# The scatters of expert gates: one generator that hands them out at GpSimd's pace, in turns between four sets

## The chip, the cores and the metric

The kernel runs on one core of one Trainium2 chip. The metric is the device time of one execution in microseconds (us). It was timed three times before the change: 3150.28, 3154.98 and 3162.14 us, a median of 3154.98 us. One further execution was profiled; all rows below come from it.

## What is computed

Two transformer blocks over 256 tokens of width 2048, all in float32. The first block's second half is a layer that picks, for each token and each of 8 heads, 16 of 16384 experts:

```python
scores = einsum('thpc,hpnc->thpn', q, sub_keys)      # 8 heads, 2 halves, 128 keys
vals, idx = lax.top_k(scores, 16)
cand = vals[..., 0, :, None] + vals[..., 1, None, :]
top_vals, top_c = lax.top_k(cand.reshape(T, 8, 256), 16)
experts = i1 * 128 + i2                              # 128 experts for each token
gates = softmax(top_vals)
y = einsum('ted,td->te', expert_down[experts], x)    # then gelu, times gates
y = einsum('ted->td', ... expert_up[experts])
```

The kernel does not gather the experts' rows. It multiplies all 16384 experts with all tokens, and then multiplies the activations with a gate that is zero wherever a token did not choose the expert.

## The kernel before, in words

The matrix products run as one long list in `run` (L268): each gemm is cut into weight tiles of 1 MB, each tile into two subtiles. A subtile is loaded by SP (`raw`), split into a rounded part on ACT (`whi`) and a remainder on DVE or GpSimd (`wlo`), and multiplied by TensorE. The program is written out while it is built, in one order for each engine: each subtile's instructions, then one call of `round` (L225), which advances each active generator of each lane by one step. What a generator issues in a step lands on its engine's queue at that place. Each engine runs its queue in order; semaphores are set by the framework from the data. The planner has a clock of its own for each engine, `vt`, which `Meter` (L173) moves on by an estimated time for each instruction. DMAs move no clock.

The gates go like this. `query` and `choose` (L982, L1023) compute, for each of 4 groups of two heads (`g`) and 2 halves of the tokens (`tt`), the 16 best experts and their gates: 8 sets of 32 columns, one after another on DVE. `scatter` (L1091) then issues, for each of a set's 32 columns, one indirect DMA (L1096) that adds 128 gates to a table in DRAM. There are four tables, `gd[g % 2, tt]`; sets 1 to 4 write four different ones, sets 5 to 8 the same four again. An accumulating scatter reads and writes its table, so each waits until the last scatter on the same table has landed. The lane `rows` runs up to four such generators at once, and each gives one scatter in each round.

The expert layer has two parts. `s1` multiplies the 16 chunks of 1024 experts with the tokens (256 subtiles); `activate` writes the activations to DRAM. `s2` multiplies the gated activations with the second weights. Between them stands `weigh` (L1118): for each chunk GpSimd loads the activations (L1124) and four pieces of the gate tables (L1127), adds two of them (L1130), and nine rounds later DVE multiplies activations and gates (L1133). The first `weigh` generators are started when the fourteenth chunk of `s1` has been activated (L940), and only when all 256 scatters have been handed out (L1121). GpSimd's queue holds first the scatters, then loads and additions of chunk 0, then those of chunk 1. In DVE's queue the multiplications stand between the `wlo` of the last subtiles of `s1`. When all scatters are handed out, `share` goes back to 2.0 (L1102); from then on a `wlo` may go to GpSimd when DVE's clock runs 2 us ahead.

Of the kernel before, what the change touches and what calls it, by code (L numbers as in the profile page):

```python
# [10 lines left out]
I32 = mybir.dt.int32  # L11
U32 = mybir.dt.uint32
AF = mybir.ActivationFunctionType
OP = mybir.AluOpType
# [4 lines left out]
T = 256  # L19
# [5 lines left out]
CAND = [(0, 1, 16), (1, 1, 8), (2, 1, 5), (3, 1, 4), (4, 1, 3), (5, 3, 2), (8, 8, 1)]  # L25
NCAND = 50
CLAMP = 2.0
MATCH, PACE = 0.09, 2.0
SWA_ORDER = [0, 3, 1, 4, 2, 5, 6, 9, 7, 10, 8, 11]


# [177 lines left out]
class Build:  # L209
# [364 lines left out]
    def body(self):  # L574
        from contextlib import ExitStack
        with ExitStack() as ctx:
            tc = self.tc
            self.cp = ctx.enter_context(tc.tile_pool(name="cp", bufs=1))
            self.sm = ctx.enter_context(tc.tile_pool(name="sm", bufs=1))
            self.wp = ctx.enter_context(tc.tile_pool(name="wp", bufs=1))  # L580
            self.xp = ctx.enter_context(tc.tile_pool(name="xp", bufs=1))
            self.np = ctx.enter_context(tc.tile_pool(name="np", bufs=1))
            self.wk = ctx.enter_context(tc.tile_pool(name="wk", bufs=1))
            self.hgt, self.hgs = None, deque()
            self.ph = None
            self.ps = ctx.enter_context(tc.tile_pool(name="ps", bufs=1, space=PSUM))
            self.dr = ctx.enter_context(tc.tile_pool(name="dr", bufs=1, space=DRAM))
            ctx.enter_context(tc.manual_schedule())
            self.xs = Slots(self.xp, "xt", 3)
            self.nb = Slots(self.np, "nb", 7)  # L590
            self.lane("evac", 2, 2)
            self.lane("main", 8, 1)
            self.lane("tail", 4, 4)
            self.lane("attn", 2, 1)
            self.lane("choose", 1, 1, True)
            self.lane("top", 2, 2, True)
            self.lane("rows", 4, 2)
            self.program()
            self.phase(None)

# [282 lines left out]
    def peer(self, hn, st):  # L883
        nc, ins = self.nc, self.ins
        nch = NE // CH
        x = self.x_of(hn)
        topn = set()
        done = dict(rows=0)
        at, acts, ws = {}, {}, []
        s2 = [0]  # L890

        def begin():
            assert not any(self.lanes[l]["queue"] or self.lanes[l]["active"] for l in ("attn", "tail"))
            self.phase("query")
            self.share = 1e9
            p = self.pp
            st["keys"] = self.nb.take([128, 2048])
            nc.gpsimd.dma_start(st["keys"], ins["keys"])
            st["top"] = self.nb.take([128, 3, 2, 8, 2, 16])
            st["pick"] = self.nb.take([128, 768])  # L900
            st["pk"] = st["pick"][:, :512].rearrange("p (t i n) -> p t i n", t=2, i=2)
            st["v"], st["ixf"] = st["top"][:, 0], st["top"][:, 1]
            st["ix"] = st["top"][:, 2].bitcast(U32)
            self.eqs = Slots(p, "eq", 2)
            st["oh"] = self.xs.take([128, 4096])
            st["q"], st["qT"], st["sc"] = (deque(st["oh"][:, 512 * i:512 * i + 512] for i in r)
                                           for r in ((0, 1, 2, 3), (4, 5), (6, 7)))

        def q_evac(g, acc):
            for tt in range(2):  # L910
                self.until(lambda: st["q"])
                q = st["q"].popleft()
                nc.scalar.activation(q, acc[tt], AF.Copy, scale=st["rh"][:, tt:tt + 1])
                self.add("top", self.query(g, tt, q, st, topn))
                self.add("choose", self.choose(g, tt, st, topn, done))

        def s1_evac(c):
            def f(g, acc):
                if c not in acts:
                    acts[c] = self.dr.tile([8, 128, T], F32, name=f"act{c}")  # L920
                self.until(lambda: "rrow" in st)
                sg = self.tmp([128, 2, T])
                for n in range(2):
                    nc.scalar.activation(sg[:, n], acc[n][:, T:], AF.Copy)
                self.add("evac", activate(c, g % 4, acc, sg))
            return f

        def activate(c, j, acc, sg):

            yield 1  # L930
            for n in range(2):
                nc.vector.tensor_tensor(sg[:, n], sg[:, n], acc[n][:, :T], op=OP.add)
            nc.vector.tensor_tensor(sg, sg, st["rrow"][:, None, :].to_broadcast([128, 2, T]), op=OP.mult)
            yield 1
            nc.scalar.activation(sg, sg, AF.Gelu_apprx_tanh)
            yield 1
            nc.scalar.dma_start(acts[c][2 * j:2 * j + 2].rearrange("a p t -> p a t"), sg)
            if j == 3:
                ws.append(self.weigh(c, acts, at, st, done, s2))
                if c >= nch - 3:  # L940
                    while ws:
                        self.add("main", ws.pop(0))

        def s2_evac(c):
            def f(g, acc):
                for tt in range(2):
                    hs = self.h[:, tt, 512 * g:512 * g + 512]
                    nc.vector.tensor_tensor(hs, hs, acc[tt], op=OP.add)
                if c == nch - 1 and "after_peer" in st:
                    for tt in range(2):  # L950
                        self.add("main", st["after_peer"](g, tt))
            return f

        def s2_done(c):
            def f():
                at[c].free()
                s2[0] = c + 1
            return f

        def s1_done():  # L960
            for hf in hn:
                hf.free()
            self.nb.give(st["pick"])
            if "rows_2" in st:
                self.add("main", st["rows_2"]())

        def x_at(c, kc):
            return (at[c], kc) if c in at and at[c].n[kc] == 2 else None

        g = [Gemm("query", ins["wq"], 0, range(4), 4, x, q_evac, None, begin)]  # L970

        def s1(c):
            return Gemm("s1", ins["wd"], 0, range(4 * c, 4 * c + 4), 2, x, s1_evac(c),
                        s1_done if c == nch - 1 else None, turned=True)

        def s2g(c):
            return Gemm("s2", ins["wu"], 8 * c, range(4), 2,
                        lambda kc: x_at(c, kc), s2_evac(c), s2_done(c))

        return g + [s1(c) for c in range(nch)] + [s2g(c) for c in range(nch)]  # L980
# [42 lines left out]
    def choose(self, g, tt, st, topn, done):  # L1023

        nc, p = self.nc, self.pp
# [10 lines left out]
        for src, dst in ((v, cand), (ixf, ec)):  # L1036
            o = 0
# [15 lines left out]
        tv, tf, tp, e, gs = tt4[:, 0], tt4[:, 1], tt4[:, 2].bitcast(U32), tt4[:, 3], tt4[:, 4]  # L1053
# [32 lines left out]
        nc.vector.tensor_scalar(ix, e.rearrange("p a b -> p (a b)"), 128.0, self.c("row"), op0=OP.mult, op1=OP.add)  # L1086
        if g == 3 and tt == 1:
            self.nb.give(st["top"])
        self.add("rows", self.scatter(g, tt, st, done))

    def scatter(self, g, tt, st, done):  # L1091

        nc = self.nc
        gd = st["gd"][g % 2, tt].rearrange("e (t o) -> (e t) o", o=1)
        for c in range(32 * g, 32 * g + 32):
            nc.gpsimd.indirect_dma_start(  # L1096
                out=gd, out_offset=bass.IndirectOffsetOnAxis(ap=st["pk"][:, tt, 0, c:c + 1].bitcast(I32), axis=0),
                in_=st["pk"][:, tt, 1, c:c + 1], in_offset=None, compute_op=OP.add)
            yield 1
        done["rows"] += 32  # L1100
        if done["rows"] == T:
            self.share = 2.0  # L1102

    def zero_gates(self, st):

# [605 lines left out]
```

## Time and profile before

| | us |
|---|---|
| median of three runs | 3154.98 |
| the profiled execution, whole | 3151.58 |
| its span, first to last instruction | 3149.8 |
| TensorE busy | 3056.1 (97%) |
| DVE busy | 2008.5 (64%) |
| ACT busy | 1429.5 (45%) |
| GpSimd (POOL) busy | 744.8 (24%) |

An engine's busy time is a sum over stages with different limits, so a mostly idle engine can still be the one that the others wait for in one stage. TensorE is idle for some 94 us of the span; where that falls is read from the windows.

### The profile page before, as it was taken

The numbers are of one execution on the slowest core, as the hardware profiler recorded it, in microseconds if no ns is written. First come the engines' busy times: TensorE is split into PE (matmuls) and PEld (weight loads), VectorE is DVE, ScalarE is ACT, GpSimd is POOL, SyncE is SP. The second block draws the span as 40 slices with busy tenths as digits, with TensorE's granted clock in tenths as the row PEclk, the third lists the DMA queues.
The fourth block names the chain that finished last, engine by engine and source line by source line (L and its number), as shares of the span: only waits on it lengthen the run. The fifth ranks groups of instructions, "written<-read, shape, count | busy, mean of one in ns | idle before, by whom it ended". The sixth has DMA issues, their size and how long they took to land.

```text
span 3149.8 us, 39414 instructions
## 1 busy us (share of the span) xinstructions
PE 3056.1 (97%) x15388; PEld 2574.3 (82%) x15388; DVE 2008.5 (64%) x2908; ACT 1429.5 (45%) x1918; POOL 744.8 (24%) x503
## 2 busy tenths in 40 slices
PE   8999999999999995699999999999999999999998
PEld 6888888888888884678888888877888888888887
DVE  4555668999555552677676765655757555555565
ACT  4445444555444442334444444554545444444443
POOL 3011201687665764343122110000111000000000
PEclk9999999999999997899999999999999999999999
DMA  9556954677777775788777755454444455555554
GB/s 347 220 174 222 329 179 167 193 201 228 213 213 213 212 215 131 258 298 290 278 255 274 272 201 197 174 204 147 168 168 174 171 191 194 193 187 188 192 194 147
DMA packets 157530, 667.32 MB, mean 212 GB/s; under 512 B 48944, under 2 KB 65756, under 8 KB 90144
## 3 DMA queue, kind: packets, MB, share of 16 engines
q1 hardware_dynamic: 77984, 551.64, 49.1%
q0 software_dynamic: 61808, 96.32, 12.4%
q10 hardware_dynamic: 17552, 16.85, 1.6%
q8 instruction: 121, 1.98, 0.2%
q14 instruction: 65, 0.53, 0.0%
HBM read 612.16 MB, written 54.94 MB: 212 GB/s over the span
## 4 chain that ended last, share of the span: by engine, by line
PE 70%; DMA 16%; POOL 7%; DVE 4%; issue 3%; ACT 1%; DVEq 0%; POOLq 0%; SPq 0%; ACTq 0%
PE acc L195 65%; DMA gates<-nb 12%; POOL gates L1096 5%; PE aux L195 5%; DMA nb<-gates 3%; DVE wlo L195 2%; DVE nb L195 1%; POOL nb L1127 0%; ACT whi L195 0%; POOL nb L195 0%; DVE xt L195 0%; DMA raw<-in_w 0%; DMA raw<-in_wu 0%; DVE tt L195 0%; DVE tmp L195 0%
## 5 line engine op out<-in xcount | busy, mean ns | idle before, releaser
L195 DVE TENSOR_TENSOR wlo<-raw,whi 128x1024 fp32r<-128x1024 f32 x1038 | 1299.8, 1255 | 838.2 <-ACT whi L195 829.2
L195 PE MATMUL acc<-whi,xt 128*128 128x512 f32 x5248 | 1666.7, 394 | 1.9 <-ACT whi L195 1.6
L195 ACT ACTIVATE whi<-raw 128x1024 fp32r<-128x1024 f32 x1040 | 1094.3, 1057 | 944.3 <-PE acc L195 853.6
L195 PEld LDWEIGHTS acc<-whi,xt 128*128 128x128 f32 x5248 | 987.1, 188 | 215.1 <-issue 6.0
L195 PE MATMUL acc<-wlo,xt 128*128 128x512 f32 x2624 | 1024.7, 391 | 5.9 <-POOL wlo L195 4.1
L195 PE MATMUL acc<-xt,whi 128*128 128x512 f32 x3072 | 772.3, 393 | 3.1 <-DVE xt L195 3.1
L195 PEld LDWEIGHTS acc<-xt,whi 128*128 128x128 f32 x3072 | 554.6, 189 | 103.1 <-DVE xt L195 3.3
L195 PEld LDWEIGHTS acc<-wlo,xt 128*128 128x128 f32 x2624 | 494.2, 188 | 108.9 <-DVE wlo L195 5.4
L1096 POOL DMA_INDIRECT gates<-nb x256 | 474.5, 1853 | 411.4 <-DMA gates<-nb 204.7
L195 PEld LDWEIGHTS acc<-xt,wlo 128*128 128x128 f32 x3072 | 420.9, 191 | 91.9 <-DVE wlo L195 62.2
L195 PE MATMUL acc<-xt,wlo 128*128 128x256 f32 x3072 | 431.3, 283 | 60.1 <-DVE wlo L195 60.0
L195 ACT ACTIVATE tmp<-tmp 128x512 f32<-128x512 f32 (+5 forms) x84 | 46.5, 554 | 216.0 <-DVE tmp L195 215.8
L195 POOL TENSOR_TENSOR nb<-nb,nb 128x1024 f32<-128x1024 f32 (+1 forms) x34 | 93.8, 2777 | 201.9 <-DMA nb<-gates 169.9
L195 DVE TENSOR_TENSOR nb<-nb,nb 128x1024 f32<-128x1024 f32 (+2 forms) x42 | 54.6, 1308 | 68.8 <-POOL nb L195 68.8
L1127 POOL DMA_DIRECT2D nb<-gates x64 | 56.8, 920 | 172.3 <-DVE nb L195 131.4
L195 ACT ACTIVATE tmp<-acc 128x256 f32<-128x256 f32 x128 | 41.8, 378 | 105.2 <-PE acc L195 105.2
L195 DVE TENSOR_TENSOR h<-h,acc 128x512 f32<-128x512 f32 x136 | 86.8, 679 | 0.0
L195 ACT ACTIVATE p<-p 128x128 f32<-128x128 f32 x88 | 39.4, 449 | 81.8 <-DVE p L195 81.8
L195 ACT ACTIVATE xt<-aux 128x512 fp32r<-128x512 f32 (+2 forms) x70 | 39.7, 584 | 76.3 <-PE aux L195 76.0
L195 POOL TENSOR_TENSOR tmp<-nb,const 128x64 f32<-128x64 f32 x32 | 11.2, 379 | 231.3 <-ACT nb L195 231.3
L195 DVE TENSOR_TENSOR xt<-nb,xt 128x1024 fp32r<-128x1024 f32 x48 | 62.6, 1307 | 2.5 <-ACT xt L195 2.5
L195 ACT ACTIVATE xt<-nb 128x1024 fp32r<-128x1024 f32 x48 | 50.3, 1053 | 30.2 <-PE acc L195 30.2
(232 smaller groups left out, 1267.6 us busy)
## 6 DMA issues: line engine op xcount, KB each, us to landing
raw<-in_wd SPq DMA_DIRECT2D x128, 1024.0 KB
raw<-in_wu SPq DMA_DIRECT2D x128, 1024.0 KB
raw<-in_wm SPq DMA_DIRECT2D x128, 1024.0 KB
raw<-in_w SPq DMA_DIRECT2D x87, 1024.0 KB
gates<-const POOLq DMA_DIRECT2D x32, 1024.0 KB
raw<-in_wo SPq DMA_DIRECT2D x32, 1024.0 KB
nb<-gates POOLq DMA_DIRECT2D x64, 512.0 KB
raw<-in_wq SPq DMA_DIRECT2D x16, 1024.0 KB
```

The source lines that it names most:

```text
L195: return f(*a, **k)
L1096: nc.gpsimd.indirect_dma_start(out=gd, out_offset=bass.IndirectOffsetOnAxis(ap=st["pk"][:, tt, 0, c:c + 1].bitcast(I32), axis=0), in_=st[" ...
L1127: nc.gpsimd.dma_start(g[:, :, 128 * tt:128 * tt + 128], st["gd"][hf, tt][CH * c:CH * c + CH].rearrange("(a p) t -> p a t", p=128))
```

## The change

One generator takes the place of eight. `choose` puts its finished set on a list, `st["chosen"]`, instead of starting a generator. The one generator is started with the expert layer, in a lane of width 1. In each round it takes finished sets into up to four turns, brings GpSimd's planned clock up to at least 2 us behind TensorE's, and hands out scatters, one from each turn in order, until that clock is 1.9 us ahead of TensorE's; each scatter moves the clock by 1.9 us. `share` goes back to 2.0 when it has handed out all.

```diff
-MATCH, PACE = 0.09, 2.0
+MATCH, PACE, SCATTER = 0.09, 2.0, 1.9
...
-            self.lane("rows", 4, 2)
+            self.lane("rows", 1, 1)
...
+            st["chosen"] = deque()
+            self.add("rows", self.scatter(st, done))
...
-        self.add("rows", self.scatter(g, tt, st, done))
-
-    def scatter(self, g, tt, st, done):
-
-        nc = self.nc
-        gd = st["gd"][g % 2, tt].rearrange("e (t o) -> (e t) o", o=1)
-        for c in range(32 * g, 32 * g + 32):
-            nc.gpsimd.indirect_dma_start(
-                out=gd, out_offset=bass.IndirectOffsetOnAxis(ap=st["pk"][:, tt, 0, c:c + 1].bitcast(I32), axis=0),
-                in_=st["pk"][:, tt, 1, c:c + 1], in_offset=None, compute_op=OP.add)
-            yield 1
-        done["rows"] += 32
-        if done["rows"] == T:
-            self.share = 2.0
+        st["chosen"].append((g, tt))
+
+    def scatter(self, st, done):
+
+
+        nc, vt = self.nc, self.vt
+        turns = deque()
+        while done["rows"] < T:
+            while st["chosen"] and len(turns) < 4:
+                g, tt = st["chosen"].popleft()
+                turns.append((g, tt, st["gd"][g % 2, tt].rearrange("e (t o) -> (e t) o", o=1),
+                              deque(range(32 * g, 32 * g + 32))))
+            vt["POOL"] = max(vt["POOL"], vt["PE"] - CLAMP)
+            while turns and vt["POOL"] - vt["PE"] < SCATTER:
+                g, tt, gd, left = turns.popleft()
+                c = left.popleft()
+                nc.gpsimd.indirect_dma_start(
+                    out=gd, out_offset=bass.IndirectOffsetOnAxis(ap=st["pk"][:, tt, 0, c:c + 1].bitcast(I32), axis=0),
+                    in_=st["pk"][:, tt, 1, c:c + 1], in_offset=None, compute_op=OP.add)
+                vt["POOL"] += SCATTER
+                done["rows"] += 1
+                if left:
+                    turns.append((g, tt, gd, left))
+            yield 1
+        self.share = 2.0
```

## Rows read from the trace of the kernel before

**Rows 1.** The page, chain that ended last: shares of the span by line.

```profile
PE acc L195 65%; DMA gates<-nb 12%; POOL gates L1096 5%; PE aux L195 5%; DMA nb<-gates 3%; DVE wlo L195 2%; DVE nb L195 1%; POOL nb L1127 0%; ACT whi L195 0%; POOL nb L195 0%; DVE xt L195 0%; DMA raw<-in_w 0%; DMA raw<-in_wu 0%; DVE tt L195 0%; DVE tmp L195 0%
```

**Rows 2.** Windows: stretch, length, busy PE, PEld, DVE, ACT, POOL, clock, DMA, GB/s.

```profile
1100.00:1150.00 50.00, 50.00 (x289) 44.02 (x288) 27.05 (x30) 23.66 (x32) 34.03 (x19) 1.00 0.76 210
...
1200.00:1225.00 25.00, 24.60 (x140) 21.24 (x138) 7.41 (x8) 8.54 (x12) 10.77 (x8) 1.00 0.51 137
1225.00:1250.00 25.00, 0.00 (x0) 0.00 (x0) 0.00 (x0) 0.00 (x0) 14.68 (x12) 0.56 0.23 37
1250.00:1275.00 25.00, 4.46 (x16) 3.62 (x16) 6.97 (x6) 5.90 (x8) 8.99 (x7) 0.57 0.71 222
1275.00:1300.00 25.00, 11.11 (x56) 9.87 (x57) 16.02 (x12) 3.08 (x4) 12.27 (x8) 0.65 0.56 186
```

**Rows 3.** Timeline, TensorE: start, duration, operation, count, idle before and its releaser.

```profile
1219.81 2.00 PE L195 MATMUL acc<-xt,whi 128*128 128x512 f32 x8
...
1222.60 2.00 PE L195 MATMUL acc<-xt,whi 128*128 128x512 f32 x8
1265.69 2.07 PE L195 MATMUL acc<-xt,wlo 128*128 128x256 f32 x8 [41.09 <-DVE wlo L195]
...
1288.89 2.08 PE L195 MATMUL acc<-xt,wlo 128*128 128x256 f32 x8 [18.74 <-DVE wlo L195]
...
1332.63 1.12 PE L195 MATMUL acc<-xt,wlo 128*128 128x256 f32 x8
```

**Rows 4.** Timeline, DVE, at the same place.

```profile
1211.76 1.24 DVE L195 TENSOR_TENSOR wlo<-raw,whi 128x1024 fp32r<-128x1024 f32 x1 [1.51 <-ACT whi L195]
1261.15 3.35 DVE L195 TENSOR_TENSOR nb<-nb,nb 128x1024 f32<-128x1024 f32 x1 [48.14 <-POOL nb L195]
...
1282.21 3.35 DVE L195 TENSOR_TENSOR nb<-nb,nb 128x1024 f32<-128x1024 f32 x1 [14.06 <-POOL nb L195]
```

**Rows 5.** Timeline, GpSimd: the last scatter, then chunks 0 and 1.

```profile
1243.53 1.54 POOL L1096 DMA_INDIRECT gates<-nb  x1 [1.62 <-DMA gates<-nb]
1244.51 1.54 POOL L1124 DMA_DIRECT2D nb<-act  x1
...
1258.78 4.63 POOL L195 TENSOR_TENSOR nb<-nb,nb 128x1024 f32<-128x1024 f32 x2 [9.18 <-DMA nb<-gates]
...
1279.85 4.63 POOL L195 TENSOR_TENSOR nb<-nb,nb 128x1024 f32<-128x1024 f32 x2 [12.08 <-DMA nb<-gates]
```

**Rows 6.** Timeline, DVE: the last instruction of the first, second and eighth set.

```profile
523.57 0.24 DVE L195 TENSOR_SCALAR nb<-tt,const 128x32 int32<-128x32 f32 x1
...
549.64 0.57 DVE L195 TENSOR_SCALAR nb<-tt,const 128x32 int32<-128x32 f32 x1
...
764.03 0.24 DVE L195 TENSOR_SCALAR nb<-tt,const 128x32 int32<-128x32 f32 x1
```

**Rows 7.** Groups, GpSimd, from 524, 564.5, 632, 895.5, 1062.4, 1118.6, 1218: busy, mean, idle.

```profile
L1096 POOL DMA_INDIRECT gates<-nb x8 | 13.3, 1657 | 188.3 <-DVE nb L195 164.9 <-DMA gates<-nb 23.4
...
L1096 POOL DMA_INDIRECT gates<-nb x24 | 45.0, 1873 | 24.6 <-DMA gates<-nb 21.0 <-issue 3.4 <-DVE tmp L195 0.3
...
L1096 POOL DMA_INDIRECT gates<-nb x38 | 76.6, 2017 | 15.5 <-issue 9.8 <-DMA gates<-nb 5.4 <-DVE cand L195 0.3
...
L1096 POOL DMA_INDIRECT gates<-nb x21 | 37.1, 1767 | 14.4 <-DMA gates<-nb 10.5 <-issue 4.0
...
L1096 POOL DMA_INDIRECT gates<-nb x24 | 43.7, 1822 | 12.4 <-DMA gates<-nb 7.9 <-issue 4.6
...
L1096 POOL DMA_INDIRECT gates<-nb x30 | 57.2, 1906 | 37.8 <-DMA gates<-nb 34.8 <-issue 3.1
...
L1096 POOL DMA_INDIRECT gates<-nb x9 | 13.8, 1538 | 17.9 <-DMA gates<-nb 17.9
```

**Rows 8.** GpSimd, 560 to 1500: all its scatters as a group; gaps without a wait.

```profile
L1096 POOL DMA_INDIRECT gates<-nb x249 | 462.7, 1858 | 227.1 <-DMA gates<-nb 185.3 <-issue 41.2 <-DVE tmp L195 0.3
...
POOL gates L1096 <- issue: 41.2, 135, 0.3
```

## The prediction

> **What bounds the kernel now.** I read the shares of the chain that ended last first. TensorE's accumulations hold 65% of it, but the scatters, as DMA and as issues, hold 12% and 5% [rows 1]: over a stretch of the span the end is set by GpSimd, an engine that the page shows 24% busy. The windows say where that costs anything. TensorE is busy without a gap beside the scatters at 1100 to 1150, and then does nothing at 1225 to 1250 and little until 1300, with the granted clock at 0.56 to 0.65 there, near the lower of its two levels, 1.2 of 2.4 GHz, after TensorE has stood still [rows 2]. So the scatters cost nothing while they run; what costs is that they end late.
>
> TensorE's timeline shows the price. One subtile of `s1` takes 1222.60 - 1219.81 = 2.79 us. After the one that ends at 1224.60 it waits 41.09 us for a `wlo`, does one subtile, waits 18.74 us for the next, and then runs evenly to the end of `s1` at 1332.63 + 1.12 = 1333.75 [rows 3]. From 1265.69 on there are 17 subtiles. Without a wait they would end at 1224.60 + 17 x 2.79 = 1272.0; `s1` is **61.7 us late**.
>
> The two `wlo` wait in DVE's queue, behind multiplications of `weigh` that wait for GpSimd: 48.14 us for chunk 0, 14.06 us for chunk 1 [rows 4]. GpSimd ends its last scatter at 1243.53 + 1.54 = 1245.07, issues the loads of chunk 0 at once, adds from 1258.78, loads chunk 1 and adds from 1279.85 [rows 5]. The chunk-1 chain ends last: TensorE's second restart, 1288.89, stands 43.8 us behind the end of the scatters. Call that end E. As long as DVE waits there, a microsecond on E is a microsecond on the kernel, so the lateness is E - (1245.1 - 61.7) = **E - 1183.4**, and nothing is to be gained from an E below 1183.
>
> **The change part by part.** The queues of TensorE, DVE and ACT keep their order: scatters move no clock that these follow, the start of `weigh` hangs on the fourteenth chunk, and the one rule that could hold it longer (all 256 handed out) is met far ahead. By plan the scatters are handed out over 256 x 1.9 = 486 us from the first set at 523.57 [rows 6], to about 1010; the first `weigh` is started some twelve rounds, 33 us, ahead of the multiplication that DVE reaches after 1213.00 [rows 4], near 1180. If that cover failed, the loads would stand later behind the scatters, which is a loss only from an E below 1180. The return of `share` moves from some 90 us after the last set to about 1010. Between these DVE is busy about half of the time (27.05 of 50 us at 1100 [rows 2]), so no `wlo` would have gone to GpSimd: nothing. Number and data of the scatters stay, and no wait is added.
>
> What changes is the order of 256 scatters in GpSimd's queue, and with it how far apart two scatters on one table stand. Before, a round hands out one of each active set, and a set lasts 32 rounds, 89 us, while sets come 34 us apart ((764.03 - 523.57) / 7 [rows 6]): mostly two or three tables in turn. Following the rounds I count about 17 alone, 98 in twos, 141 in threes, and never four.
>
> The trace prices each kind, as busy plus idle over count [rows 7]. **Alone**: the first eight 1.66 + 23.4 / 7 = 5.0 us, the last nine 31.7 / 9 = 3.5 us, these while the DMA engines are quiet. **Twos**: (45.0 + 24.6 + 57.2 + 37.8) / 54 = 3.05 us. **Threes**: (76.6 + 15.5 + 37.1 + 14.4 + 43.7 + 12.4) / 83 = 2.41 us. **Fours** do not occur. Below they are bounded by issue alone: mean duration 1.86 and a gap of 41.2 / 135 = 0.30 without a wait, 2.16 us [rows 8]. Above I take the threes' 2.41, since a scatter whose table was used one place further back should not wait more; that four in flight delay each other is no contradiction in terms, and stands as a rival. In threes the wait for landing is still 5.4 to 10.5 us for 21 to 38 scatters; the fourth place gives about 2.2 us more. But back to back the durations are longer: 2.02 us in the stretch with the fewest waits, which with 0.30 makes 2.32 [rows 7]. I take **2.3 us**.
>
> Now the new counts. Set 1 is alone for 26.1 us (549.64 - 523.57), later sets come 35.7 us apart (214.39 / 6) [rows 6]. At one scatter in 1.9 us that is 14 alone, then 19 in twos, 19 in threes, 9 in fours until set 1 is done, 10 in threes until set 5 comes. Left are then about 10.7, 20.1, 26.4 and 32. From there four turns are full until only three sets are left: 10.7 + 9.4 + 6.3 + 5.6 = 32 rounds, 128 scatters. As a set enters only when one is used up, in order, the four turns are always four tables. At the end 32 in threes, 19 in twos, 6 alone. In all **20 alone, 38 in twos, 61 in threes, 137 in fours**.
>
> The sum: 14 x 5.0 = 70; 6 alone at the end at 4.3 (between the two prices) = 26; 38 x 3.05 = 116; 61 x 2.41 = 147; 137 x 2.3 = 315; together 674 us. The same prices with the counts of before give 8 x 5.0 + 9 x 3.5 + 98 x 3.05 + 141 x 2.41 = 710, where the trace has 1245.1 - 524.1 = 721 us; so I scale by 1.015: 684 us, and **E = 1208**. Where the 36 us between 710 and 674 come from: 60 places in twos become fours, 60 x 0.75 = 45, and 80 in threes, 80 x 0.11 = 9; but the first set, handed out faster, stands alone for 14 places instead of 8, and the lone places, 20 for 96 us instead of 17 for 71, take 18 back (25 less 3 x 2.3).
>
> With E = 1208 the lateness is 25 us. To it comes that the loads of chunk 0 would then run beside weight loads, not on quiet DMA engines: GpSimd waited 9.18 us for chunk 0 and 12.08 for chunk 1, where DMA was busier [rows 5, 2]. I add 4 us, between 0 and 10. DVE's wait for chunk 0 nearly goes (E + 16 = 1224 against 1213 and its lead over TensorE of 1224.60 - 1213.00 = 11.6 us [rows 3, 4]); the wait for chunk 1 is **what is late next**, some 30 us at one place. Gain 61.7 - 29 = 33 us. From the profiled execution's 3151.6 that is **3119 us**; its own time lies 3.4 us below the median of the runs, which I leave inside the range.
>
> The bounds: fours at 2.16 give E = 1188 and, with the 4 us, a gain of 53, 3099 us; fours at 2.41 and 10 us for the loads give E = 1223, a gain of 12, 3140 us.
>
> **Rivals.** *All of it comes back.* E falls below 1183 if the fours cost 2.12 us or less, or if the single scatters land faster than the first eight did. For it speaks that a quarter of the stretch from 560 to 1245 is waiting for landings (185.3 of 685 us [rows 8]); against it that the bound 2.16 is a mean over durations that are longer back to back. Gain 62, 3090 us.
>
> *The landing, not the turn, sets the pace.* Four tables help only if four scatters land beside each other. If they land one after another, each delayed by the weight loads, more turns only lengthen each landing. For it: twos start 6.1 us apart on one table (2 x 3.05), threes 7.2, where one alone needs 5.0; so landings stretch with each more in flight. Against it: 38 threes in a row at 2.42 with hardly a wait. The fours would then cost 2.5 to 2.65; E = 1235 to 1256, 3142 to 3164 us, say 3148: no change that can be told.
>
> The Trainium skill, "DMA: Bandwidth & Descriptors", states in "SWDGE vs HWDGE vs iDMA" that GpSimd's DMAs have a single queue, and in "Queues, rings and completion order" that each DMA engine switches between queues only at the end of a packet. By that rule all four tables share one queue beside the weights' queue, which is what this rival needs; the trace agrees in part, with the landings that stretch from 5.0 to 7.2 us.
>
> *Slower.* The same mechanism past a point: the new order pays 18 us for its lone places at once, and must earn them in the fours. From fours at 2.58 on E passes 1245, and from about 2.70 the kernel is slower by over 0.5%. At 2.85 E is 1285 and the time 3191 us. The threes of the three stretches shown cost 2.34 to 2.45, so the chance is small.
>
> **How the numbers follow.** Forecast (fours between 2.13 and 2.47) 0.67, all of it 0.13, no change 0.15, slower 0.05. A measurement of this kernel can tell about 0.5%, 16 us, from no change; of the forecast's own share 0.03 falls below that, and of the no-change case 0.01 beyond it. So faster 0.77, same 0.17, slower 0.06. The range runs from all of it (3090, a little lower for a clock that no longer falls) to the dearest bound: 3086 to 3143.
>
> **What would show it.** In the changed trace: the first 14 scatters at about 5 us each; from about 700 to 1030 us scatters nearly back to back at 2.3 us; the last one near 1208, and right behind it the loads of chunk 0; one DVE wait for GpSimd's addition of about 30 us in place of 48 and 14; the end of `s1` near 1301 instead of 1334; everything behind it as before, only earlier. The prediction is wrong if the fours stand outside 2.16 to 2.41, if the lateness does not follow E - 1183, or if time moves behind `s1`.

## The result, and the profile after

The changed kernel takes 3115.87 us (median of four runs, 3101.4 to 3117.03) against 3155.95 us before (four runs, 3150.28 to 3162.14): 40 us or 1.3% faster by the medians. The ratio of the means is 0.9862, with a 95% interval from 0.9828 to 0.9897; 3119 us was predicted. The profiled execution took 3117.03 us, its span 3115.3 us.

The share of the scatters in the chain that ended last, the page's line as in [rows 1]:

```profile
PE acc L195 68%; POOL gates L1107 9%; PE aux L195 5%; DMA gates<-nb 4%; DMA nb<-gates 3%; DVE wlo L195 2%; DVE nb L195 1%; DVE tt L195 1%; DVE tmp L195 0%; DVE xt L195 0%; POOL nb L1140 0%; POOL nb L195 0%; ACT whi L195 0%; DMA raw<-in_w 0%; DMA raw<-in_wu 0%
```

The waits for landings went from 12% to 4% of the span, and GpSimd's issues rose from 5% to 9%: the scatters are still the chain there, but it now runs through issue instead of landing. The groups of scatters on GpSimd, in the windows where the order of the list has them alone (from 525 us), in twos (599), in threes (649), in fours (689 and, after a stretch in threes, 745), in threes (1034), in twos (1109) and alone (1165); the columns are those of [rows 7]:

```profile
L1107 POOL DMA_INDIRECT gates<-nb x14 | 25.3, 1805 | 213.4 <-DVE nb L195 164.9 <-DMA gates<-nb 48.5
...
L1107 POOL DMA_INDIRECT gates<-nb x18 | 34.0, 1887 | 16.0 <-DMA gates<-nb 12.9 <-issue 3.0
...
L1107 POOL DMA_INDIRECT gates<-nb x18 | 33.7, 1874 | 6.4 <-issue 4.6 <-DMA gates<-nb 1.8
...
L1107 POOL DMA_INDIRECT gates<-nb x9 | 21.1, 2350 | 2.7 <-issue 2.4 <-DVE eq L195 0.3
...
L1107 POOL DMA_INDIRECT gates<-nb x128 | 247.1, 1930 | 42.3 <-issue 37.5 <-DMA gates<-nb 4.5 <-DVE nb L195 0.3
...
L1107 POOL DMA_INDIRECT gates<-nb x30 | 57.0, 1900 | 17.4 <-DMA gates<-nb 11.0 <-issue 6.4
...
L1107 POOL DMA_INDIRECT gates<-nb x19 | 34.5, 1813 | 21.6 <-DMA gates<-nb 19.4 <-issue 2.1
...
L1107 POOL DMA_INDIRECT gates<-nb x7 | 11.7, 1671 | 22.6 <-DMA gates<-nb 22.3 <-issue 0.3
```

The row with 128 is the heart of the change. Of 42.3 us idle only 4.5 wait for a landing; (247.1 + 42.3) / 128 = 2.26 us for each. The two lone rows are no cheaper than before: (25.3 + 48.5) / 14 = 5.3 us, and (11.7 + 22.6) / 7 = 4.9.

TensorE's timeline at the change of parts, as in [rows 3], then DVE's, as in [rows 4], then GpSimd's, as in [rows 5]:

```profile
1229.94 1.92 PE L195 MATMUL acc<-xt,wlo 128*128 128x256 f32 x8 [4.33 <-DVE wlo L195]
1252.83 2.08 PE L195 MATMUL acc<-xt,wlo 128*128 128x256 f32 x8 [18.28 <-DVE wlo L195]
...
1296.92 1.12 PE L195 MATMUL acc<-xt,wlo 128*128 128x256 f32 x8
```

```profile
1225.39 3.35 DVE L195 TENSOR_TENSOR nb<-nb,nb 128x1024 f32<-128x1024 f32 x1 [11.40 <-POOL nb L195]
...
1246.16 3.34 DVE L195 TENSOR_TENSOR nb<-nb,nb 128x1024 f32<-128x1024 f32 x1 [13.75 <-POOL nb L195]
```

```profile
1196.61 2.02 POOL L1107 DMA_INDIRECT gates<-nb  x1 [4.62 <-DMA gates<-nb]
1198.07 1.54 POOL L1137 DMA_DIRECT2D nb<-act  x1
...
1222.97 4.70 POOL L195 TENSOR_TENSOR nb<-nb,nb 128x1024 f32<-128x1024 f32 x2 [19.64 <-DMA nb<-gates]
...
1243.79 4.63 POOL L195 TENSOR_TENSOR nb<-nb,nb 128x1024 f32<-128x1024 f32 x2 [11.78 <-DMA nb<-gates]
```

The last scatter ends at 1198.6 instead of 1245.1 us. DVE's wait for chunk 0 fell from 48.14 to 11.40 us, the one for chunk 1 stayed (14.06 before, 13.75 now), and TensorE's two waits went from 41.09 and 18.74 to 4.33 and 18.28 us. `s1` ends at 1296.92 + 1.12 = 1298.0 instead of 1333.75, 35.7 us sooner, where the two profiled executions differ by 34.6 us. So all of the gain lies there, and behind it about 1 us was lost. TensorE stops at 1229.94 - 4.33 = 1225.6 us, where it stopped at 1224.6 before, with 17 subtiles left in both: the multiplications stand at the same place in DVE's queue.

The windows show what is left of the hole, as in [rows 2]:

```profile
1225.00:1250.00 25.00, 5.22 (x19) 3.89 (x17) 10.82 (x8) 5.90 (x8) 13.22 (x10) 0.67 0.55 178
1250.00:1275.00 25.00, 22.17 (x116) 19.51 (x117) 19.19 (x19) 8.78 (x11) 6.05 (x6) 0.85 0.87 307
```

TensorE stands for most of one window of 25 us instead of two and more, and the granted clock, which falls towards its lower level of 1.2 of 2.4 GHz while it stands, is 0.67 and 0.85 there instead of 0.56, 0.57 and 0.65 over three.

### The profile page after: what moved, and what is told of

Its sections match the earlier page's. It is cut to its first block, busy times and chain, and to the rows that moved or that the text cites. A ratio compares the mean times of both kernels' runs of the same rounds, so it can differ in the third digit from the quotient of the medians.

```text
span 3115.3 us, 39413 instructions
## 1 busy us (share of the span) xinstructions
PE 3058.1 (98%) x15388; PEld 2577.5 (83%) x15388; DVE 2009.8 (65%) x2908; ACT 1428.9 (46%) x1918; POOL 764.0 (25%) x503
## 4 chain that ended last, share of the span: by engine, by line
PE 73%; POOL 10%; DMA 8%; DVE 5%; issue 3%; ACT 1%; DVEq 0%; POOLq 0%; SPq 0%; ACTq 0%
PE acc L195 68%; POOL gates L1107 9%; PE aux L195 5%; DMA gates<-nb 4%; DMA nb<-gates 3%; DVE wlo L195 2%; DVE nb L195 1%; DVE tt L195 1%; DVE tmp L195 0%; DVE xt L195 0%; POOL nb L1140 0%; POOL nb L195 0%; ACT whi L195 0%; DMA raw<-in_w 0%; DMA raw<-in_wu 0%
## 5 line engine op out<-in xcount | busy, mean ns | idle before, releaser
L195 ACT ACTIVATE whi<-raw 128x1024 fp32r<-128x1024 f32 x1040 | 1094.1, 1057 | 944.9 <-PE acc L195 852.1
L1107 POOL DMA_INDIRECT gates<-nb x256 | 491.4, 1920 | 347.0 <-DVE nb L195 165.2
(232 smaller groups left out, 1269.8 us busy)
```

The lines of the kernel that those rows point to most:

```text
L195: return f(*a, **k)
L1107: nc.gpsimd.indirect_dma_start(out=gd, out_offset=bass.IndirectOffsetOnAxis(ap=st["pk"][:, tt, 0, c:c + 1].bitcast(I32), axis=0), in_=st[" ...
```

## Experiments

The theory has two steps. First, a scatter's place costs more the fewer tables stand between two scatters on the same table, so the order alone sets E, the end of the last scatter. Second, E sets the end of `s1`, since DVE's queue stands before multiplications that wait for GpSimd's additions. Rivals were the landings (four in flight no faster than three), the pace alone, and something else that holds the change of parts.

### Two sets in turn, and three

```diff
-            while st["chosen"] and len(turns) < 4:
+            while st["chosen"] and len(turns) < 2:
```

> The kernel after with at most two sets in turn instead of four, nothing else. By the rule of the list: about 29 scatters alone, 227 in twos. Theory (the cost of a place is set by how many tables stand between two scatters on one table, and the kernel is late by E - 1183, E the end of the last scatter): 29 x 5.1 + 227 x 2.9 = 806 us, E near 1330, the first part of the expert layer 145 to 150 us late instead of 25, time 3237 to 3250 us. Rival A (what gained was the pace of the single generator, not the number of turns): time as after, 3117. Rival B (a part of E is hidden again behind later work, so that less than 1 us is paid for 1 us): under 3200.

One execution: 3219.79 us, 103 us more than the profiled execution of after, and more than the kernel before. The last scatter ends at 1308.88 + 1.54 = 1310.4 us and `s1` at 1398.8. TensorE's timeline there:

```profile
1330.91 2.08 PE L195 MATMUL acc<-xt,wlo 128*128 128x256 f32 x8 [106.88 <-DVE wlo L195]
1354.16 2.07 PE L195 MATMUL acc<-xt,wlo 128*128 128x256 f32 x8 [17.76 <-DVE wlo L195]
```

The direction and the price for a microsecond are the theory's: against the kernel before, E is 65.3 us later, the end of `s1` 65.0 and the execution 68.2 us. The number missed by some 20 us. Three groups say why, from 700 us, from 900 us, and from 1225 to 1266 us, where TensorE, ACT and DVE all stand:

```profile
L1107 POOL DMA_INDIRECT gates<-nb x66 | 119.9, 1817 | 80.2 <-DMA gates<-nb 72.2 <-issue 7.3 <-DVE wlo L195 0.3
...
L1107 POOL DMA_INDIRECT gates<-nb x63 | 114.4, 1816 | 87.9 <-DMA gates<-nb 82.1 <-issue 5.8
...
L1107 POOL DMA_INDIRECT gates<-nb x22 | 33.9, 1540 | 6.7 <-issue 6.7
```

Twos cost 3.03 and 3.21 us beside the weight loads, but (33.9 + 6.7) / 22 = 1.84 us while those engines wait, without one wait for a landing; over the whole run they average 2.91 us, as I had taken. The miss lies in the lone scatters: the last 14 came in the same quiet and took 3.3 us each, so that all 29 took 126 us where 29 x 5.1 = 148 were expected. A late end slows less than it seems.

That 22 scatters back to back took 1.54 us each also says what makes the issue longer elsewhere. It is not that the scatters follow each other closely, but what DVE does when one starts. Three scatters of the kernel after, then two instructions of DVE at the same place:

```profile
810.84 2.33 POOL L1107 DMA_INDIRECT gates<-nb  x1 [0.30 <-issue]
813.48 1.54 POOL L1107 DMA_INDIRECT gates<-nb  x1 [0.30 <-issue]
...
817.65 2.22 POOL L1107 DMA_INDIRECT gates<-nb  x1 [0.30 <-issue]
```

```profile
810.53 1.23 DVE L195 TENSOR_TENSOR wlo<-raw,whi 128x1024 fp32r<-128x1024 f32 x1 [1.51 <-ACT whi L195]
...
817.24 1.22 DVE L195 TENSOR_TENSOR wlo<-raw,whi 128x1024 fp32r<-128x1024 f32 x1
```

The first and the third scatter start while a `wlo` runs on DVE, and both end 1.41 us after that `wlo` does. The second starts while DVE stands and takes 1.54 us. So it is in the whole profile of after: all 36 scatters that start beside no DVE instruction take 1.54 to 1.56 us, 27 of them right behind another scatter, and the median of the 137 that start at least 0.15 us before the end of a `wlo` ends 1.41 us after it.

```diff
-            while st["chosen"] and len(turns) < 4:
+            while st["chosen"] and len(turns) < 3:
```

> The kernel after with at most three sets in turn. By the rule of the list about 29 alone, 41 in twos, 186 in threes. Theory: 29 x 5.1 + 41 x 2.9 + 186 x 2.4 = 713 us, E near 1235, late by 52 to 55 us instead of 25, time 3144 to 3150 us, close to the kernel before. Rival (four in flight are no faster than three, the gain came from fewer twos): E near 1205, time 3117 to 3125.

3143.88 us (3140.45 to 3149.48), a ratio to before of 0.9964 (0.9948 to 0.9981): as expected by the theory. In the profiled execution, of 3140.7 us, E is 1233.2 and `s1` ends at 1321.7. Threes cost (155.3 + 45.4) / 81 = 2.48 and (152.6 + 49.6) / 85 = 2.38 us:

```profile
L1107 POOL DMA_INDIRECT gates<-nb x81 | 155.3, 1917 | 45.4 <-DMA gates<-nb 28.3 <-issue 17.1
L1107 POOL DMA_INDIRECT gates<-nb x85 | 152.6, 1796 | 49.6 <-DMA gates<-nb 33.2 <-issue 16.2 <-DVE wlo L195 0.3
```

Three turns against four make 28 us of the 40. The fourth turn takes nearly all of the wait for landings away (33.2 us for 85 threes, 4.5 for 128 fours). That the gain came from fewer twos alone is out.

### A faster and a slower hand-out

```diff
-MATCH, PACE, SCATTER = 0.09, 2.0, 1.9
+MATCH, PACE, SCATTER = 0.09, 2.0, 1.2
```

> The kernel after with SCATTER = 1.2: the scatters are handed out faster than GpSimd can issue them. By the rule of the list about 42 alone, 181 in twos, 33 in threes, none in fours. Theory: 42 x 5.1 + 181 x 3.0 + 33 x 2.4 = 836 us less some 25 that the quiet DMA engines give back once TensorE stands, E 1325 to 1340, late by 140 to 155 us, time 3230 to 3250 us. Rival (an earlier hand-out ends earlier, whatever the order): below 3117.

One execution: 3188.26 us, 71 us slower than the profiled execution of after. The scatters handed out sooner end later, at 1277.95 + 1.54 = 1279.5. The expected sum was 57 us too long (836 - 25 = 811 us; the scatters took 754). Some 39 us of that are my count: written out from the program, the order has 31 alone, 166 in twos and 59 in threes, not 42, 181 and 33, and at the same prices these make 798 us. The rest is in the prices.

```diff
-MATCH, PACE, SCATTER = 0.09, 2.0, 1.9
+MATCH, PACE, SCATTER = 0.09, 2.0, 2.3
```

> The kernel after with SCATTER = 2.3 instead of 1.9, what a scatter in fours really takes with its gap. By the rule of the list about 17 alone, 31 in twos, 53 in threes, 155 in fours instead of 21, 37, 61, 137. Theory: handing out more slowly ends sooner, E 8 to 16 us below that of after, near 1175 to 1190, time 3097 to 3110 us. Rival (a slower hand-out ends later or at the same time): 3117 to 3150.

3100.72 us (3097.86 to 3103.87), ratio 0.9828 (0.9797 to 0.9859). E is 1172.72 + 1.54 = 1174.3, `s1` ends at 1280.1, with one wait of 8.0 us left. The hand-out 21% slower ends 24 us sooner (16 us against the second profile of after, below). Both fit a pace that matters through the order that it makes: a set that is handed out before the next one is chosen stands alone. What a place costs stayed the same: with the order written out, a scatter in fours took 2.27 us from end to end at a pace of 1.9 and at 2.3, one in threes 2.44 and 2.39, one in twos 2.90 and 2.91.

### Without the last two sets

```diff
-                nc.gpsimd.indirect_dma_start(
+                if g < 3:
+                    nc.gpsimd.indirect_dma_start(
```

> The kernel after without the 64 scatters of the last two sets, so the gates of two of the eight heads are missing from the tables; all else as after. E falls to about 1080, far below 1183. Theory: nothing is left of the lateness, the first part of the expert layer ends near 1273 instead of 1298, time 3117 - 25 = 3092 us, perhaps 4 less if the short wait for GpSimd's wlo behind it goes too. Rival (something else holds the end of that part: the loads of the chunks, GpSimd's additions): the wait for chunk 1 stays, time over 3105.

3087.85 us (3087.65 to 3088.16). The scatters end near 1057; `s1` ends at 1269.8, and of TensorE's waits for DVE 1.2 us are left; a wait of 3.8 us for a `wlo` of GpSimd stays. This is the floor: whatever is done to the scatters alone, 24 to 28 us below after (3111.83 and 3115.87 us) is all there is, and of the 68 us that they cost the kernel before the change took 40.

### The multiplications later in DVE's queue

```diff
-        yield 9
+        yield 9 if c > 1 else 17
```

> The kernel after, scatters unchanged, but the multiplications of chunks 0 and 1 stand 17 instead of 9 rounds behind the loads, 8 subtiles or 22 us later in DVE's queue. Theory (the cost is not the scatters' end itself but that DVE's queue is held in front of weights that TensorE needs): E stays near 1199, DVE's wait of 11 and 14 us goes to at most 8, TensorE's 4.3 + 18.3 us of waits go to 0 to 3, time 3093 to 3098 us. Rival (the chunks are needed by then anyway, so the wait moves to the start of the second part): 3110 to 3117 us.

3110.46 us (3104.09 to 3114.79): 1 to 5 us below the two medians measured for after (3111.83 and 3115.87), with spreads that overlap, so the expectation failed and the rival came: the wait moved to the second part. Half of the theory held: DVE's two waits are gone, and `s1` ends at 1271.1. But TensorE's timeline shows a new wait in the second part:

```profile
1301.03 0.79 PE L195 MATMUL acc<-wlo,xt 128*128 128x512 f32 x1 [17.75 <-POOL wlo L195]
```

GpSimd's queue tells whose it is:

```profile
1271.70 6.25 POOL L195 TENSOR_TENSOR nb<-nb,nb 128x1024 f32<-128x1024 f32 x2 [18.15 <-DMA nb<-gates]
...
1282.00 1.75 POOL L1140 DMA_DIRECT2D nb<-gates  x2 [1.45 <-DVE tmp L195]
1294.05 4.63 POOL L195 TENSOR_TENSOR nb<-nb,nb 128x1024 f32<-128x1024 f32 x2 [10.30 <-DMA nb<-gates]
1298.64 2.33 POOL L195 TENSOR_TENSOR wlo<-raw,whi 128x1024 fp32r<-128x1024 f32 x1
```

The planner gives one `wlo` at the change of parts to GpSimd, behind the additions of the fourth chunk. GpSimd loads, waits and adds for one chunk after another, and that chain starts at E: in this execution E is 1186.6 and the `wlo` is done at 1298.64 + 2.33 = 1301.0, 114.4 us later; in the profile of after it is done at 1313.6, 115.0 us behind its E of 1198.6. The edit did not shorten that chain. TensorE, no longer held in `s1`, came to this `wlo` 17.75 us too early. So E has a second deadline close behind the first one: TensorE wants this `wlo` at 1283.3, which at the same distance asks for an E of about 1168. A still earlier E does not take the whole wait away: with E at 1158.2 (below) 3.3 us of it are left, with six sets 3.8. GpSimd's queue holds another `wlo` in front of the loads of chunks 2 and 3, and with six sets GpSimd waits 107.4 us for its `whi`, which comes from ACT at 1220.7 us. Ending the scatters sooner serves both; moving a multiplication in DVE's queue serves only one.

### Handing out by price

The next kernel moves the planned clock by what a place costs, and takes, of the tables not used by the last two scatters, the one with most left.

```diff
+SCATTER = {1: 5.0, 2: 3.0, 3: 2.4, 4: 2.2}
...
-                g, tt, gd, left = turns.popleft()
+                free = [x for x in turns if x[0] not in last[-min(2, len(turns) - 1):]] or turns
+                x = max(free, key=lambda x: len(x[3]))
...
-                vt["POOL"] += SCATTER
+                vt["POOL"] += SCATTER[len(turns)]
```

> The generator of after with two rules changed. The planned clock moves by what a place costs with that many sets in turn (5.0 alone, 3.0 in twos, 2.4 in threes, 2.2 in fours) instead of 1.9, and of the tables not used by the last two scatters that with most left comes next, so that the four sets end together. By this rule some 6 alone, 12 in twos, 15 in threes and over 210 in fours: 6 x 5.2 + 12 x 2.9 + 15 x 2.4 + 223 x 2.24 = 602 us, E near 1128. Theory: chunk 0 and 1 are added long before DVE needs them, lateness 0, time as with six sets alone, 3086 to 3093 us. Rival (the handing out, which now ends near 1115 to 1130, or the loads hold the multiplications all the same): over 3105.

3153.07 us (3146.44 to 3155.58), as slow as the kernel before. The group from 1100 us shows where it went:

```profile
L1110 POOL DMA_INDIRECT gates<-nb x30 | 51.7, 1723 | 103.3 <-DMA gates<-nb 103.3
```

30 scatters at 5.2 us: they stand alone. With "most left first", one scatter of the fourth set stayed in its turn while the three new sets rotated, so the eighth set could not enter until they were used up, and then ran alone. The order, not the prices, was at fault. The clock alone, with the turns in order, tells these apart:

```diff
-            while turns and vt["POOL"] - vt["PE"] < SCATTER:
+            while turns and vt["POOL"] - vt["PE"] < 1.9:
+                vt["POOL"] += SCATTER[len(turns)]
...
-                vt["POOL"] += SCATTER
```

> The kernel after with one rule changed: the planned clock moves by what a place costs with that many sets in turn (5.0, 3.0, 2.4, 2.2) instead of 1.9; turns in order, as in after. By the rule of the list about 11 alone, 23 in twos, 35 in threes, 187 in fours. Theory: 11 x 5.2 + 23 x 2.9 + 35 x 2.4 + 187 x 2.25 = 629 us, E 1150 to 1160, handed out by about 1137, loads for chunk 1 added by 1210, so nothing is late: 3086 to 3096 us. Rival (e5's time shows that a slower hand-out holds up the loads, not that 30 scatters stood alone at its end): 3140 or more.

3087.74 us (3087.29 to 3089.23), ratio to before 0.9794 (0.9769 to 0.9820): the floor. E is 1156.16 + 2.04 = 1158.2, and TensorE waits 1.7 us for DVE and 3.3 us for GpSimd's `wlo`. It beats both kernels, after by 24 us on the same chip.

The last wait was tried with each of the two, by giving `share` back later:

```diff
-        self.share = 2.0
...
                 s2[0] = c + 1
+                self.share = 2.0
```

> The kernel of e5 with share going back to 2.0 only when the first chunk of the second part is done, so no wlo stands behind GpSimd's additions at the change of parts. Theory: the wait of TensorE for a wlo of GpSimd, 3.8 us with six sets, goes and no other takes its place: 3 to 4 us less than e5. Rival (DVE then is late itself): as e5 or up to 5 us more.

> The kernel of e9, and share goes back to 2.0 only when the first chunk of the second part is done, so no wlo stands in GpSimd's queue at the change of parts. Theory: the wait of 4 to 5 us for a wlo of GpSimd goes, 3 to 4 us less than e9, 3082 to 3092 us. Rival (DVE, which has to do that wlo, is late by as much): as e9.

On the first it gave 3149.68 us (3142.63 to 3155.85) against 3153.07, on the second **3083.58 us** (3080.00 to 3086.82) against 3087.74. Each median is 3 to 4 us lower, as expected; the spreads of the first pair overlap widely, those of the second do not, and with a ratio of 0.9777 (0.9749 to 0.9804) it is the fastest kernel here. Why is not shown. The wait for GpSimd is gone in both traces, but another took its place, which was the rival: on the first kernel TensorE waits 10.88 us for a `wlo` of DVE where it waited 11.63 us for GpSimd's, on the second 3.9 us in all for DVE where it waited 3.3 for GpSimd and 1.7 for DVE. The profiled executions differ by 2.3 us the wrong way and by 1.2 us the right way.

### The kernel after once more

> The kernel after, unchanged, beside the two others on one chip, with a second profile of it. Theory (its time varies with E, since the lone scatters land at different times in each execution): 3101 to 3117 us, and E of this profile differs from 1198.6 by as much as the time differs from 3117. Rival (the time varies for another reason): E the same within 2 us at another time.

3111.83 us (3104.96 to 3120.71). The profiled execution took 3105.4 us, 11.6 less than the first. E is 1188.96 + 1.54 = 1190.5, 8.1 us sooner, and GpSimd waited 14.89 us for the loads of chunk 0 instead of 19.64; `s1` ends at 1287.2. The order is the same in both. Of the 8.1 us, 1.4 stand ahead of the first scatter, and at the fourteenth, the last of the lone ones, it is already 7.8: the landings of lone scatters differ from execution to execution, and the time goes with them. It goes by more than E alone, 11.6 us, since the loads of chunk 0 were shorter too. Two kernels that end the scatters well ahead spread by 2 us or less (pace by price in order, six sets), after by 16; but the fastest kernel, with its E at 1164.0, spread by 6.8, and that is not explained.

### All runs side by side

From the profiled execution of each, in us; "rest" is the time less the end of `s1`:

| kernel | E | end of `s1` | end of `s1` - E | time | rest |
|---|---|---|---|---|---|
| six sets | 1057.5 | 1269.8 | 212.3 | 3088.0 | 1818 |
| pace by price, in order | 1158.2 | 1269.9 | 111.7 | 3087.3 | 1817 |
| the same, `share` later | 1164.0 | 1271.4 | 107.4 | 3086.1 | 1815 |
| pace 2.3 | 1174.3 | 1280.1 | 105.8 | 3098.7 | 1819 |
| multiplications later | 1186.6 | 1271.1 | 84.6 | 3104.1 | 1833 |
| after, again | 1190.5 | 1287.2 | 96.7 | 3105.4 | 1818 |
| after | 1198.6 | 1298.0 | 99.4 | 3117.0 | 1819 |
| three turns | 1233.2 | 1321.7 | 88.5 | 3140.7 | 1819 |
| before | 1245.1 | 1333.8 | 88.7 | 3151.6 | 1818 |
| pace by price, most left | 1252.2 | 1326.6 | 74.4 | 3153.6 | 1827 |
| the same, `share` later | 1256.6 | 1329.6 | 73.0 | 3155.9 | 1826 |
| pace 1.2 | 1279.5 | 1367.5 | 88.0 | 3188.3 | 1821 |
| two turns | 1310.4 | 1398.8 | 88.4 | 3219.8 | 1821 |

From E = 1233 up `s1` ends 88 us behind E within 1 us, but for the two kernels with the most-left rule. Their TensorE stops at 1238.7 us (the first of the two) instead of 1225.6 and has 12 subtiles left instead of 17: their multiplications stand later in DVE's queue, most likely since `weigh` waits until all scatters are handed out and these kernels hand out the last ones late. The 88 us hold for multiplications at one place. Below E = 1233 the loads run beside weight loads and take 8 to 17 us longer, until the end of `s1` meets its floor of 1270. The rest is 1815 to 1821 us; the exceptions are the three kernels where TensorE waits 10.9 to 17.75 us for a `wlo` behind `s1`.

## Why the prediction was right, point by point

**What bounds the kernel.** Shown. With the multiplications in place, the table gives 1 us for 1 us over a range of 77 us in E, and the kernel without the last two sets gives the floor at 1269.8, where 1272.0 was worked out.

**The counts.** 20 alone, 38 in twos, 61 in threes and 137 in fours were worked out; the order as written out has 20, 35, 60 and 141. For the kernel before the count was worse: 17 alone, 98 in twos and 141 in threes were worked out, the order has 18, 109 and 129.

**The price of the fours.** 2.3 us was taken; 128 cost 2.26, the nine early ones (21.1 + 2.7) / 9 = 2.64 with a mean duration of 2.35, all 137 together 2.29. They lie where I put them between 2.16 and 2.41, and hardly anything waits there. The reason given for more than 2.16, that the issue is longer back to back, was wrong: its length goes by DVE, which is busy for 23.14 of 23.90 us beside the nine early ones (mean duration 2.35 us) and for 172.64 of 289.30 beside the 128 (1.93 us). Nor is 2.16 a bound: with DVE at rest 22 scatters took 1.84 us each. That 2.3 came out close is not owed to that reason: it was read from a stretch in which DVE worked too.

**E.** 1208 predicted, 1198.6 and 1190.5 measured. The sum of the prices alone was 674 us, to E = 1198; the step that failed is the scale of 1.015, taken from the misfit of the same prices on the kernel before (710 against 721 us). That misfit came from the wrong count: with 18, 109 and 129 places the same prices make 9 x 5.0 + 9 x 3.5 + 109 x 3.05 + 129 x 2.41 = 720 us, and there is nothing to scale.

**The loads.** 4 us were added, the first profile shows 10.7 (99.4 - 88.7) and the second 8.0. The mechanism, weight loads beside the loads of chunk 0, was right and the size too small by half. The two errors nearly cancel, by luck: 29 us late were predicted, 25.0 (1298.0 against 1273.0 undisturbed, 1225.6 + 17 x 2.79) came.

**What is late next.** One wait of 30 us for chunk 1 was forecast; there are two, 11.40 and 13.75 us. The sum is near, the split is not: slower loads of chunk 0 make chunk 0 late too.

**The threshold.** E = 1183 for no loss at all was too generous; with 1174.3 `s1` is still 8 to 10 us late, with 1158.2 and with 1164.0 (the fastest kernel, `s1` to 1271.4) it is not, or by less than 2 us. The slower loads again.

**The rivals.** Four in turn leave 4.5 us of wait in 128 scatters, so the rival of the landings, which had 0.15 of the chances, is out, and with it the slower case. The Trainium skill ("DMA: Bandwidth & Descriptors", "SWDGE vs HWDGE vs iDMA") states that GpSimd's DMAs have a single queue; the trace shows that this does not keep four such scatters from overlapping, at 2.26 us each where one alone took 5.3.

## What to carry to other kernels

Where operations must wait for their predecessor on the same target, count for each how many others stand between the two: here the order in the queue set the end, with the same operations. Handing work out faster than the engine can take it can end it later, since what is at hand early is queued without a partner; a planner's clock should move by what a place costs in the company that it has. And a hole in the busiest engine is best followed through the in-order queue before it: a wait moved away from one queue can appear in front of the next weight on another.

## What the runs showed of the hardware

An accumulating scatter of 128 elements took 1.54 us to issue when no DVE instruction ran at its start; one that started 0.15 us or more before the end of a `wlo` on DVE ended 1.41 us after it (the median of 137), which made means of 1.93 us in fours and 2.35 us in the stretch where DVE was busiest. The traces show the times; what in the chip ties the two engines together is not shown. From the start of a lone scatter to the start of the next one on its table were 3.2 us on quiet DMA engines ([rows 5]: 1.54 and a wait of 1.62; 3.2 to 3.4 at the end of the run with two turns) and 4.9 to 5.3 us beside the weight loads. Two executions of one program differed by 8.1 us in E, 6.4 of them in the landings of the first 13 lone scatters; with the loads behind them they differed by 11.6 us, where the eight times of this kernel span 19 us.
